# Linear memory over two blocks of 256 prompt tokens with a carried state, in place of one block of 512

## The chip, the cores and the metric

The kernel runs on one core of a Trainium2 chip. A core has a matrix engine (TensorE, PE in the profile; its weight loads are shown apart as PEld), a vector engine (VectorE, DVE), an activation engine (ScalarE, ACT), a general engine (GpSimd, POOL) and SyncE (SP), which here only issues transfers. TensorE writes to a small memory of its own, PSUM, of which this kernel uses one pool of four buffers for side work ("aux") and another for the large products ("mm"). The metric is the device time of one execution, in microseconds (us); the smaller the better.

## The reference

The kernel computes one layer of a streaming encoder for 512 prompt frames and 64 sample frames at width 1024: a feed-forward half step, a mixer of two branches, another feed-forward half step. One of the branches is a linear memory with four heads of 256. The reference runs it over chunks with a state C (256 x 256), n and a running maximum m:

```python
bcum = jnp.cumsum(lf, axis=-1)
dmat = jnp.where(causal, bcum[..., :, None] - bcum[..., None, :] + li[..., None, :], -jnp.inf)
inter = bcum + m[..., None]
m_t = jnp.maximum(inter, jnp.max(dmat, axis=-1))
w_inter = jnp.exp(inter - m_t)
s = jnp.einsum('bhtd,bhsd->bhts', q, k) * jnp.exp(dmat - m_t[..., None])
num = w_inter[..., None] * jnp.einsum('bhtd,bhde->bhte', q, C) + jnp.einsum('bhts,bhse->bhte', s, v)
den = w_inter * jnp.einsum('bhtd,bhd->bht', q, n) + jnp.sum(s, axis=-1)
h = num / jnp.maximum(jnp.abs(den), jnp.exp(-m_t))[..., None]
...
decay = jnp.exp(b_last + m - m_new)
w_s = jnp.exp(g_s - m_new[..., None])
C_new = decay[..., None, None] * C + jnp.einsum('bhs,bhsd,bhse->bhde', w_s, k, v)
```

The chunk length is free: any split of the tokens gives the same h and the same last state, since what the earlier chunks hold reaches a later one through C and n. The prompt starts with C = 0; the 64 sample frames bring a state of their own. After this h is normalised over the 256 entries of a head, gated, and multiplied by the branch's output matrix.

## The kernel before, in words

All products are done in three passes. A float32 operand is split in a high part (rounded to the matmul's float32 form, fp32r) and the remainder; `mm3` (L137) issues high x high, high x low and low x high as three matmuls into one PSUM bank. So each product of two tensors needs four tiles: for W they are Wh and Wl, for the keys kwh and kwl, for v vh and vl. The high part is mostly written by ScalarE (L147), the low part by VectorE (a subtraction, L150 or L153).

Tokens lie in blocks of 128: blocks 0 to 3 are the prompt, block 4 the 64 sample frames. The heads' loop (`for h in range(4)`) does for every head:

- `ml_kq` (L1986): the projections of k and q (four "gemms" of 24 matmuls a row half, weights streamed from memory), each followed by a short convolution over time on VectorE (U) and a SiLU on ScalarE (qf). `turn5` transposes k and v by TensorE, five blocks at a time, four in one aux bank and the sample's in the next; the sinks write kwh, kwl (scaled by the token's weight) and vh, vl. The v turns wait until the hidden blocks of the head before have been issued, since vh and vl have one buffer.
- `ml_decay` (L2035): the row of running maxima is spread over all partitions by two matmuls (mr, sel), copied to Mb, and ScalarE makes the decays D of each block by an exponential, masked by GpSimd. The exponential is in another function table than SiLU, so a table load stands between them.
- `ml_early`, `weights(b)`: for key block b the scores against all queries from that block on, W = (k q) * D. Over 512 prompt tokens these are 512, 384, 256 and 128 columns wide for b = 0 to 3, six matmuls each, and 64 for the sample.
- `ml_late`: `state(e)` sums k and v over the four prompt blocks (12 matmuls of 258 columns: 256 of v, one of ones for n, one unused) and over the sample block (3), for each half e of the key dimension. `hidden(b)` multiplies W and v: for block b one term from each of the blocks 0 to b, three matmuls a term, and the result is copied to hf by ScalarE. The sample's has one term and two of the old state (ch, cl, with q scaled in qsc). Then `norm` on hf, and `back(e)` transposes hf and multiplies by the gate og.

The order on TensorE is written out by hand. `Order` (L42 to L84) holds a clock that every matmul advances by its estimated length; `later(dt, fn)` puts a piece of side work on a heap with a due time, and between the gemms' matmuls the pieces that are due are issued, with a space of 380 ns between two of them in the heads. So the side work of one head falls among the gemms of the same and the next head, and the due times (`10000 + 2100 * b` and the like) set where. After head 3 come the projections of three branch gates (FILL), then what is left on the heap, then gate 7 and the output matrix of the branch. The order of the other engines comes from a scheduler that takes the emitted order and priorities (`high_priority`, `hot`); each engine runs its list strictly in turn.

The four aux banks are handed out in rotation by `bank()` (L122): a request waits until the last reader of the buffer four requests ago is done.

Before the heads, `gate_rows` (L1391) computes the sums of the forget gates, the running maxima and the exponentials for all heads on four partitions, in small pieces among the attention's projections (about 430 to 530 us in the profile). It ends by transposing the 128-row tile `rows` into `tcol`, which holds per token and head the columns: a weight for D, a weight for the keys, exp(-m).

Of the kernel before, what the change touches and what calls it, by code (L numbers as in the profile page):

```python
# [17 lines left out]
P = 128  # L18
# [68 lines left out]
def tile_layer(ctx: ExitStack, tc: tile.TileContext, ins, outs):  # L87
# [1274 lines left out]
    scol = gp.tile([4, 8], F32, name="scol")  # L1362
    tcol = gp.tile([P, 5, 12], F32, name="tcol")
    tstack = ExitStack()
# [16 lines left out]
    POOL.memset(tcol[:, 4, :], 1.0)  # L1381
    gdone = []
    vf0, kf0, qf0 = (slot(F32, tp, t) for t in ("vf0", "kf0", "qf0"))

# [6 lines left out]
    def gate_rows():  # L1391
# [25 lines left out]
        SP.dma_start(outs["m"][:, 1:2], mt[:, T - 1:T])  # L1417
        for i, (a, b) in enumerate(((0, NP_), (NP_, T))):
            ts(scol[:, 4 + i:5 + i], mrow[:, b - 1:b], -1.0, None, ALU.mult)
            yield act(rows[32:36, a:b], arow[:, a:b], AF.Exp, bias=scol[:, 4 + i:5 + i])  # L1420
# [9 lines left out]
        for b in range(5):  # L1430
            w = min(P, T - b * P)
            ps = bank()
            transpose(ps[:w, :P], rows[:, b * P:b * P + w], ident)
            yield DVE.tensor_copy(tcol[:w, b, :].rearrange("p (g h) -> p g h", h=4),
                                  ps[:w, :96].rearrange("p (g r) -> p g r", r=32)[:, :, 0:4])
        gdone.append(1)
# [598 lines left out]
    def ml_decay(h, st):  # L2035

        mb, mb2 = bank(), bank()
        pick = sel[:, h:h + 1].to_broadcast([P, P])
        mm(mb, pick, mr[:, :NP_], True, True)
        mm(mb2[:, 0:130], pick, mr[:, NP_:], True, True)  # L2040
        Mb = mp.tile([P, T], F32, tag="Mb", name=nm("Mb"))
        wdb = mp.tile([P, 66], F32, tag="wdb", name=nm("wdb"))
        with tc.high_priority(offset=120):
            act(Mb[:, :NP_], mb)
            act(Mb[:, NP_:], mb2[:, 0:64])
            act(wdb, mb2[:, 64:130])
# [8 lines left out]
        D = st["D"] = {}  # L2055

        def decays():

            for b in (4, 0, 1, 2, 3):
                s0 = b * P  # L2060
                n, w = (NP_ - s0, P) if b < 4 else (NS, NS)
                d = D[b] = mp.tile([P, n], F32, tag=f"D{b}", name=nm("D"))
                with tc.issue_after(order["silu"].ins):
                    order["exp"] = act(d[:w, :], Mb[:w, s0:s0 + n], AF.Exp, scale=-1.0, bias=tcol[:w, b, h:h + 1])

                POOL.affine_select(out=d[:w, 0:w], in_=d[:w, 0:w], pattern=[[1, w]], compare_op=ALU.is_ge, fill=0.0,
                                   base=0, channel_multiplier=-1)
            with tc.issue_after(order["exp"].ins):
                act(ch, c0v)
            tt(cl, c0v, f(ch), ALU.subtract)  # L2070

        later(6000, decays)

    def ml_early(h, st):
# [15 lines left out]
        def weights(b):  # L2090
            s0 = b * P
            n, w = (NP_ - s0, P) if b < 4 else (NS, NS)
            ps, d = bank(), D[b]
# [15 lines left out]
        for b in range(5):  # L2109

            later(10000 + 2100 * b if h == 3 else 11000 + 2600 * b, lambda b=b: weights(b))

    def ml_late(h, st):
        W, (c0, ch, cl), wdb, qs_ = st["W"], st["C"], st["wdb"], st["qs"]
        mv = mp.tile([P, 5, 2], F32, tag="mv", name=nm("mv"))
        dn = mp.tile([P, 5, 2], F32, tag="dn", name=nm("dn"))

        def state(e):

            ce = slice(e * P, (e + 1) * P)  # L2120
# [6 lines left out]
            SP.dma_start(outs["pC"][h, :, e, :], cn)  # L2127
            ps = bank()
            mm3(ps[:, :258], kwh[:, 4, ce], kwl[:, 4, ce], vh[:, 4, :], vl[:, 4, :], True, True)
# [238 lines left out]
```

## Time and profile before

| | us |
|---|---|
| median of 3 runs | 1546.58 |
| lowest, highest | 1545.94, 1548.52 |
| the profiled execution | 1547.03 |
| its span, first to last instruction | 1544.8 |
| TensorE busy in it | 1528.6 |
| VectorE busy | 1170.6 |
| ScalarE busy | 880.9 |
| GpSimd busy | 197.2 |

The granted clock of TensorE was 0.999 of full speed in that execution. The lines of the profile shown below are from it. A line of the list of instructions reads: start in us from the beginning of the span, duration in us, engine, source line, operation, output tile <- input tiles, sizes, and how many like it follow each other; in square brackets, where the engine stood idle before it, for how long and what ended it. TensorE's matmuls overlap: the distance from one start to the next is the pace, the duration is longer. L133 is the helper that issues matmuls, L143 transposes, L147 ScalarE's activations, L150, L153 and L157 VectorE's two-operand and scalar operations. Tile names carry no numbers, and an instruction is known by the tiles that it writes and reads: `aux<-qk,s` are the scores of `weights`, `aux<-vh,W` hidden blocks, `aux<-vh,kwh` the state, `aux<-ident,vf` a turn of v, `aux<-ident,qf` a turn of k, `aux<-ident,hf` the turn back, `mm<-...` the gemms.

### The profile page before, as it was taken

Reading aid. Unit: us, or ns where it says so; the run is one execution under the profiler, and the core shown is the slowest. Engines: PE = TensorE matmul, PEld = TensorE weight load, DVE = VectorE, ACT = ScalarE, POOL = GpSimd, SP = SyncE. Lnnn points to the kernel's source line nnn. Section 1 sums busy time; section 2 is a strip of 40 time slices with the busy share of each in tenths; the row PEclk is TensorE's granted clock in tenths of the full one; section 3 lists DMA queues with packets and bytes.
Section 4 is the critical chain, followed back from the end, with each engine's and each line's share of the span. In section 5 each row is a group of like instructions: output and inputs, shape, how many; then the busy total and the mean of one; then the engine's idle time right before and its main releaser. Section 6 shows DMA issues by size and latency. Waiting matters only on the chain.

```text
span 1544.8 us, 29439 instructions
## 1 busy us (share of the span) xinstructions
PE 1528.6 (99%) x11563; PEld 1513.4 (98%) x11563; DVE 1170.6 (76%) x2222; ACT 880.9 (57%) x1684; POOL 197.2 (13%) x370
## 2 busy tenths in 40 slices
PE   9999999999999999999999999999999999999998
PEld 9999999999999999999999999999999999999997
DVE  7877778776898767887677577775788888787765
ACT  7545446534666557777864877753456454557332
POOL 1000000100200015544200321102120000001000
PEclk9999999999999999999999999999999999999999
DMA  8322223524544449687544965542653223217333
GB/s 246 109 104 89 96 96 102 144 81 142 150 145 148 145 176 234 151 212 165 140 108 154 275 152 131 130 132 83 202 121 104 109 83 110 83 66 188 88 110 113
DMA packets 81075, 209.23 MB, mean 135 GB/s; under 512 B 9385, under 2 KB 23081, under 8 KB 80937
## 3 DMA queue, kind: packets, MB, share of 16 engines
q1 hardware_dynamic: 64936, 168.36, 32.2%
q0 software_dynamic: 14848, 37.30, 13.5%
q8 instruction: 90, 1.47, 0.4%
q10 hardware_dynamic: 1152, 1.70, 0.3%
q14 instruction: 49, 0.39, 0.1%
HBM read 170.89 MB, written 22.22 MB: 125 GB/s over the span
## 4 chain that ended last, share of the span: by engine, by line
PE 79%; DVE 9%; ACT 5%; DMA 3%; issue 3%; POOL 1%; SPq 0%; ACTq 0%; DVEq 0%; POOLq 0%
PE mm L133 67%; PE aux L133 11%; PE aux L143 1%; DVE wl L150 1%; ACT wh L147 1%; DMA s<-in_xT 1%; DVE s L150 1%; DVE sc L1608 1%; DVE s L153 1%; DVE o L150 1%; DVE U L153 1%; ACT sc L147 1%; DVE sc L157 1%; DMA wr<-in_w_in 1%; DVE kl L150 1%
## 5 line engine op out<-in xcount | busy, mean ns | idle before, releaser
L133 PE MATMUL mm<-s,wh 128*128 128x288 f32 (+2 forms) x3494 | 713.4, 298 | 1.0 <-DVE s L150 0.7
L133 PEld LDWEIGHTS mm<-s,wh 128*128 128x128 f32 x3494 | 558.7, 189 | 3.8 <-issue 0.9
L133 PE MATMUL mm<-s,wl 128*128 128x288 f32 (+2 forms) x1737 | 512.7, 295 | 0.0
L133 PEld LDWEIGHTS mm<-s,wl 128*128 128x128 f32 x1737 | 327.1, 188 | 0.2 <-DVE wl L150 0.2
L147 ACT ACTIVATE wh<-wr 128x1024 fp32r<-128x1024 f32 (+2 forms) x126 | 116.8, 935 | 108.3 <-PE mm L133 59.8
L133 PE MATMUL mm<-tx,wh 128*128 128x288 f32 x778 | 158.4, 296 | 0.0
L133 PEld LDWEIGHTS mm<-tx,wh 128*128 128x128 f32 x778 | 124.9, 188 | 0.0
L150 DVE TENSOR_TENSOR wl<-wr,wh 128x1024 fp32r<-128x1024 f32 (+2 forms) x87 | 90.8, 1053 | 36.6 <-ACT wh L147 36.5
L133 PE MATMUL mm<-tx,wl 128*128 128x288 f32 x383 | 113.0, 295 | 0.7 <-DVE wl L150 0.7
L976 ACT ACTIVATE wh<-wt 128x1024 fp32r<-128x1024 f32 x53 | 56.2, 1060 | 88.9 <-DVE wt L150 88.9
L150 DVE TENSOR_TENSOR wl<-wt,wh 128x1024 fp32r<-128x1024 f32 x53 | 64.8, 1222 | 52.6 <-ACT wh L976 52.6
L150 DVE TENSOR_TENSOR wl<-wu,wh 128x1024 fp32r<-128x1024 f32 x50 | 61.2, 1223 | 21.6 <-ACT wh L976 21.6
L223 POOL DMA_DIRECT2D s<-s x16 | 13.7, 855 | 495.0 <-ACT s L147 252.1
L133 PEld LDWEIGHTS mm<-tx,wl 128*128 128x128 f32 x383 | 72.0, 188 | 0.9 <-DVE wl L150 0.9
L147 ACT ACTIVATE h<-h 128x288 f32<-128x288 f32 x80 | 34.9, 437 | 65.2 <-DVE h L150 65.1
L976 ACT ACTIVATE wh<-wu 128x1024 fp32r<-128x1024 f32 x50 | 52.9, 1058 | 32.7 <-PE mm L133 32.5
L150 DVE TENSOR_TENSOR wl<-ws,wh 128x1024 fp32r<-128x1024 f32 x53 | 64.6, 1219 | 0.1
L150 DVE TENSOR_TENSOR ws<-wu 128x1024 f32<-128x1024 f32 x53 | 64.5, 1216 | 0.0
L133 PE MATMUL mm<-h,wh 128*128 128x256 f32 (+2 forms) x296 | 60.2, 294 | 0.0
L976 ACT ACTIVATE ah<-wu 128x512 fp32r<-128x512 f32 x53 | 33.4, 631 | 44.4 <-PE mm L133 41.3
L976 ACT ACTIVATE wh<-ws 128x1024 fp32r<-128x1024 f32 x53 | 55.8, 1052 | 0.7 <-PE mm L133 0.4
L147 ACT ACTIVATE sc<-sc,mx 128x128 f32<-128x128 f32 (+4 forms) x72 | 40.3, 560 | 25.1 <-DVE mx L1608 24.7
(420 smaller groups left out, 3609.0 us busy)
## 6 DMA issues: line engine op xcount, KB each, us to landing
wu<-in_w_gu SPq DMA_DIRECT2D x80, 512.0 KB, 4.4
wr<-in_w_in SPq DMA_DIRECT2D x46, 512.0 KB, 4.1
wl<-in_w_in POOLq DMA_DIRECT2D x38, 512.0 KB, 6.5
wr<-in_w_dn SPq DMA_DIRECT2D x34, 512.0 KB, 3.5
wu<-in_w_in SPq DMA_DIRECT2D x26, 512.0 KB, 4.7
wr<-in_w_dn SPq DMA_DIRECT2D x18, 384.0 KB, 3.5
s<-s POOLq DMA_DIRECT2D x16, 288.0 KB, 3.8
wr<-in_w_ap SPq DMA_DIRECT2D x8, 512.0 KB, 3.5
```

What stands on the lines that cost most here:

```text
L133: PE.matmul(out, lhsT, rhs, start=start, stop=stop, **kw)
L143: PE.transpose(out, in_, idn)
L147: return ACT.activation(out, in_, func, **kw)
L150: return (eng or DVE).tensor_tensor(out, a, b, op=op)
L153: return DVE.scalar_tensor_tensor(out=out, in0=a, scalar=s, in1=b, op0=op0, op1=op1)
L157: return (eng or DVE).tensor_scalar(out=out, in0=a, scalar1=s1, scalar2=s2, op0=op0, **kw)
L223: return POOL.dma_start(lo, src, accum_op=ALU.add)
L976: self.last = ACT.activation(hi, src, AF.Copy)
L1608: DVE.tensor_tensor_reduce(out=out, in0=ps, in1=g, op0=ALU.add, op1=ALU.min, scale=-1.0, scalar=3e38, accum_out=acc)
```

## The change

The prompt is treated as two blocks of 256 tokens (NC = 256). Within a block the scores and hidden products are as before, so the weights are 256 and 128 columns wide in each of the two blocks, and a hidden block has one or two terms. What the first 256 tokens give to the second goes through the state: `first(e)` sums k and v over token blocks 0 and 1 into cf, which is split into cfh and cfl; `carried(b)`, for b = 2 and 3, multiplies the queries by it (6 matmuls of 258 columns) and ScalarE copies the result to hc with a factor per token; hidden 2 and 3 add hc as they leave PSUM, on VectorE. The final state is g * cf plus the sum over token blocks 2 and 3 (`second(e)`), with the factor g from one more exponential a head; the sample's part of the state is a piece of its own (`sample(e)`). In `gate_rows` the weights of the keys are taken relative to the maximum at the end of their own block, the factor per token is one more exponential of 256 columns, and `tcol` and its copies are 16 wide rather than 12 (the copy reads 128 columns rather than 96).

The pieces' due times change too: scores and hidden blocks come later, and state sums are six pieces a head in place of two.

```diff
-    tcol = gp.tile([P, 5, 12], F32, name="tcol")
+    tcol = gp.tile([P, 5, 16], F32, name="tcol")
...
+    NC = NP_ // 2
...
-        for i, (a, b) in enumerate(((0, NP_), (NP_, T))):
+        yield act(rows[96:100, NC:NP_], mrow[:, NC:NP_], AF.Exp, bias=mrow[:, NC - 1:NC], scale=-1.0)
+        for i, (a, b) in enumerate(((0, NC), (NC, NP_), (NP_, T))):
             ts(scol[:, 4 + i:5 + i], mrow[:, b - 1:b], -1.0, None, ALU.mult)
             yield act(rows[32:36, a:b], arow[:, a:b], AF.Exp, bias=scol[:, 4 + i:5 + i])
...
             for b in (4, 0, 1, 2, 3):
                 s0 = b * P
-                n, w = (NP_ - s0, P) if b < 4 else (NS, NS)
+                n, w = (NC - s0 % NC, P) if b < 4 else (NS, NS)
...
+            with tc.issue_after(order["exp"].ins):
+                order["exp"] = act(g, Mb[:, NP_ - 1:NP_], AF.Exp, scale=-1.0, bias=Mb[:, NC - 1:NC])
...
         def weights(b):
             s0 = b * P
-            n, w = (NP_ - s0, P) if b < 4 else (NS, NS)
+            n, w = (NC - s0 % NC, P) if b < 4 else (NS, NS)
...
-            later(10000 + 2100 * b if h == 3 else 11000 + 2600 * b, lambda b=b: weights(b))
+            later(11200 + 2000 * b if h == 3 else 12600 + 2500 * b, lambda b=b: weights(b))
...
-        def state(e):
+        def first(e):
             ce = slice(e * P, (e + 1) * P)
             ps = bank()
-            for s in range(4):
-                mm3(ps[:, :258], kwh[:, s, ce], kwl[:, s, ce], vh[:, s, :], vl[:, s, :], s == 0, s == 3)
+            for s in range(2):
+                mm3(ps[:, :258], kwh[:, s, ce], kwl[:, s, ce], vh[:, s, :], vl[:, s, :], s == 0, s == 1)
+            with tc.high_priority(offset=100):
+                act(cf[:, e, :], ps[:, :258])
+            act(cfh[:, e, :], cf[:, e, :])
+            tt(cfl[:, e, :], cf[:, e, :], f(cfh[:, e, :]), ALU.subtract)
+
+        def second(e):
+            ce = slice(e * P, (e + 1) * P)
+            ps = bank()
+            for s in range(2, 4):
+                mm3(ps[:, :258], kwh[:, s, ce], kwl[:, s, ce], vh[:, s, :], vl[:, s, :], s == 2, s == 3)
             cn = mp.tile([P, 258], F32, tag="cn", name=nm("cn"), bufs=2)
             with tc.high_priority(offset=100):
-                act(cn, ps[:, :258])
+                stt(cn, cf[:, e, :], st["g"][:, 0:1], ps[:, :258], ALU.mult, ALU.add)
             SP.dma_start(outs["pC"][h, :, e, :], cn)
...
+        def carried(b):
+            ps = bank()
+            for e in range(2):
+                qh, ql = (x[:, b * P:(b + 1) * P] for x in st["q"][e])
+                mm3(ps[:, :258], qh, ql, cfh[:, e, :], cfl[:, e, :], e == 0, e == 1)
+            with tc.high_priority(offset=100):
+                act(hc_[:, b - 2, :], ps[:, :258], scale=tcol[:, b, 12 + h:13 + h])
...
-                          vh[:, s, :], vl[:, s, :]) for s in range(b + 1)]
+                          vh[:, s, :], vl[:, s, :]) for s in range(b // 2 * 2, b + 1)]
...
             with tc.high_priority(offset=60):
-                act(hf_[:w, b, :], ps[:w, :258])
+                if b in (2, 3):
+                    tt(hf_[:, b, :], ps[:, :258], hc_[:, b - 2, :], ALU.add)
+                else:
+                    act(hf_[:w, b, :], ps[:w, :258])
...
         for e in range(2):
-            later(5500 + 1800 * e, lambda e=e: state(e))
+            later(4500 + 1300 * e, lambda e=e: first(e))
+            later(7000 + 2400 * e, lambda e=e: second(e))
+            later(8200 + 2400 * e, lambda e=e: sample(e))
+        for b in (2, 3):
+            later(14000 + 2000 * (b - 2) if h == 3 else 16300 + 2600 * (b - 2), lambda b=b: carried(b))
         for b in range(5):
-            later(16000 + 1800 * b if h == 3 else 19500 + 2200 * b, lambda b=b: hidden(b))
+            later(17000 + 1800 * b if h == 3 else 20500 + 2200 * b, lambda b=b: hidden(b))
```

More of the change, by code (lines that the diff above doesn't have):

```diff
@@ L1434, in gate_rows @@
             yield DVE.tensor_copy(tcol[:w, b, :].rearrange("p (g h) -> p g h", h=4),
-                                  ps[:w, :96].rearrange("p (g r) -> p g r", r=32)[:, :, 0:4])
+                                  ps[:w, :P].rearrange("p (g r) -> p g r", r=32)[:, :, 0:4])
         gdone.append(1)
@@ L2055, in ml_decay @@
         D = st["D"] = {}
+        st["g"] = g = mp.tile([P, 1], F32, tag="g", name=nm("g"), bufs=2)
         def decays():
@@ L2116, in ml_late, with sample @@
         dn = mp.tile([P, 5, 2], F32, tag="dn", name=nm("dn"))
-        def state(e):
+        cf = mp.tile([P, 2, 258], F32, tag="cf", name=nm("cf"))
+        cfh, cfl = (mp.tile([P, 2, 258], F32R, tag=t, name=nm(t)) for t in ("cfh", "cfl"))
+        hc_ = mp.tile([P, 2, 258], F32, tag="hc", name=nm("hc"))
+        def first(e):
             ce = slice(e * P, (e + 1) * P)
             ps = bank()
-            for s in range(4):
-                mm3(ps[:, :258], kwh[:, s, ce], kwl[:, s, ce], vh[:, s, :], vl[:, s, :], s == 0, s == 3)
+            for s in range(2):
[9 more added lines that the diff above has]
+                mm3(ps[:, :258], kwh[:, s, ce], kwl[:, s, ce], vh[:, s, :], vl[:, s, :], s == 2, s == 3)
             cn = mp.tile([P, 258], F32, tag="cn", name=nm("cn"), bufs=2)
             with tc.high_priority(offset=100):
-                act(cn, ps[:, :258])
+                stt(cn, cf[:, e, :], st["g"][:, 0:1], ps[:, :258], ALU.mult, ALU.add)
             SP.dma_start(outs["pC"][h, :, e, :], cn)
+        def sample(e):
+            ce = slice(e * P, (e + 1) * P)
             ps = bank()
```

## The prediction

> **What bounds the kernel now.** I read the page first (busy shares, then the chain), then the table by stretches over the heads, then the lists of single instructions of TensorE, ScalarE and VectorE at the places the change touches.
>
> ```profile
> PE 1528.6 (99%) x11563; PEld 1513.4 (98%) x11563; DVE 1170.6 (76%) x2222; ACT 880.9 (57%) x1684; POOL 197.2 (13%) x370
> ...
> PE 79%; DVE 9%; ACT 5%; DMA 3%; issue 3%; POOL 1%; SPq 0%; ACTq 0%; DVEq 0%; POOLq 0%
> ```
> ```profile
> 860.00:900.00 40.00, 39.84 (x306) 39.21 (x305) 27.18 (x55) 33.88 (x77) 8.69 (x22) 1.00 0.94 255
> 900.00:950.00 50.00, 50.00 (x392) 49.31 (x391) 37.37 (x106) 38.94 (x93) 10.05 (x27) 1.00 0.52 125
> 950.00:1000.00 50.00, 50.00 (x389) 49.48 (x387) 38.05 (x101) 35.43 (x83) 10.35 (x26) 1.00 0.54 130
> 1000.00:1040.00 40.00, 40.00 (x311) 39.72 (x311) 27.70 (x63) 23.60 (x46) 2.83 (x6) 1.00 0.47 145
> ```
>
> TensorE is busy 99% of the span and 79% of the chain. In the second block (columns: length, then the busy time of TensorE, its weight loads, VectorE, ScalarE and GpSimd, the granted clock, the DMA share) the four heads lie between about 860 and 1040 us: TensorE stands still there for 0.16 of 180 us, at a clock of 1.00, while VectorE is busy 130.3 and ScalarE 131.9 of the 180. So a nanosecond of TensorE saved in the heads counts in full, and so does a wait put in front of one of its instructions. What the other engines gain or lose counts only through such a wait. Order on TensorE is fixed by hand; a wait there holds up everything behind it, the projections' gemms too.
>
> **What the change takes off TensorE.** It issues as many matmuls as before. Hidden blocks 2 and 3 lose two terms each (12 matmuls of 258 columns a head); the two carried products add 12 of 258. The state's 12 of 258 are only split in two groups of six. Nothing there. The weights of blocks 0 and 1 become narrower: six matmuls of 512 columns become 256, six of 384 become 128; blocks 2 and 3 stay. Their pace, from the start of the six to the start of what follows:
>
> ```profile
> 887.30 1.57 PE L133 MATMUL aux<-qk,s 128*128 128x512 f32 x6
> 888.70 0.40 PE L133 MATMUL mm<-s,wh 128*128 128x256 f32 x2
> ...
> 890.22 1.20 PE L133 MATMUL aux<-qk,s 128*128 128x384 f32 x6
> 891.26 0.46 PE L133 MATMUL mm<-s,wh 128*128 128x320 f32 x2
> ...
> 893.01 0.84 PE L133 MATMUL aux<-qk,s 128*128 128x256 f32 x6
> 893.69 0.46 PE L133 MATMUL mm<-s,wh 128*128 128x320 f32 x2
> ...
> 895.71 0.78 PE L133 MATMUL aux<-qk,s 128*128 128x128 f32 x6
> 896.33 0.46 PE L133 MATMUL mm<-s,wh 128*128 128x256 f32 x2
> ```
>
> 1.40 us for six of 512, 1.04 for 384, 0.68 for 256, 0.62 for 128 (the last two nearly alike: below 256 columns the pace hardly falls). A head saves (1.40 − 0.68) + (1.04 − 0.62) = 1.14 us, the four heads 4.6 us. That is the whole gain on the bounding engine.
>
> [...]
>
> **What the change adds beside TensorE.** Per head ScalarE gets cf and cfh twice, hc twice and g once in place of cn twice and hf twice, and its exponentials and W copies become narrower; VectorE gets cfl, cn and the sum hf twice each, against narrower D and W. Each is 0.3 to 0.5 us, by the rows of hf, W and D below. Per head that is some 1 to 1.5 us more on VectorE and about nothing on ScalarE; with a quarter of their time idle they cost nothing by their length. GpSimd's triangle masks keep their number and width, and SP issues the same DMAs; the one of the state leaves 1.5 us of order time later and now waits for VectorE. The weight loads queue behind it on SP; no row of TensorE in the heads waits for a load, so I take nothing.
>
> What can cost is that TensorE now meets products and banks earlier. The four aux buffers go round; the fifth request waits until the reader of the first is done. I compared, request by request, the distance to that reader before and after, in the changed order of each engine; a distance is the sum of the matmuls between, at the paces of the rows (0.12 us at 256 or 258 columns, 0.147 at 320, 0.11 for a transpose). These are the places where it gets too short.
>
> *Weights of block 2, head 0.* Weights of block 1, the carried product and the two decay matmuls come just ahead, so the group takes the buffer that weights of block 1 left 0.44 + 0.72 + 0.44 + 0.30 + 0.35 = 2.25 us earlier. Its reader, the product D on VectorE, stands in order behind two convolution steps, the low half of W and the low half of k:
>
> ```profile
> 889.71 1.68 DVE L153 SCALAR_TENSOR_TENSOR U<-R,cols,U 128x579 f32<-128x579 f32 x2
> ...
> 894.62 0.76 DVE L153 SCALAR_TENSOR_TENSOR s<-qf,s 128x576 fp32r<-128x576 f32 x1 [0.69 <-ACT s L147]
> ...
> 896.67 0.42 DVE L150 TENSOR_TENSOR W<-D,W 128x256 fp32r<-128x256 f32 x1 [0.48 <-ACT W L147]
> ...
> 899.36 0.28 DVE L150 TENSOR_TENSOR D<-aux,D 128x128 f32<-128x128 f32 x1
> ```
>
> 1.68 + 0.42 + 0.76 + 0.28 = 3.1 us and about 0.2 until a matmul's result stands (the last of six ends 0.16 after the next begins): 3.3 − 2.25 = 1.1 us of wait. It may be 0 (VectorE had 0.69 and 0.48 idle here) or 1.7. A wait of the same kind for hidden block 1 just behind it: 0.15 us (0 to 0.5).
>
> *Hidden block 2, head 0.* It takes the buffer of hidden block 0, which ended 2.37 us before; that eviction stands on ScalarE behind the table load for the decays:
>
> ```profile
> 901.34 0.63 ACT L147 ACTIVATE qf<-U 128x512 f32<-128x512 f32 x1 [0.58 <-DVE U L153]
> ...
> 902.46 1.28 ACT L147 ACT_TABLE_LOAD   x1
> 903.75 0.72 ACT L147 ACTIVATE D<-Mb,tcol 128x512 f32<-128x512 f32 x1
> 904.38 0.67 ACT L147 ACTIVATE s<-qf 128x576 fp32r<-128x576 f32 x1
> 904.96 0.36 ACT L147 ACTIVATE R<-mm 128x256 f32<-128x256 f32 x1
> 905.22 0.36 ACT L147 ACTIVATE kwh<-aux,tcol 128x128 fp32r<-128x128 f32 x1
> 905.47 0.66 ACT L147 ACTIVATE hf<-aux 128x258 f32<-128x258 f32 x2
> ```
>
> From the load's start to the end of the first hf 3.4 us, 3.15 with D at half its width; with part of qf ahead of it 3.8: 3.8 − 2.37 = 1.4 us. It is 0 if the load was through by then, 2.7 if the whole load comes on top. In the other heads that eviction stands ahead of the load, and 0.9 us are left. [...]
>
> *The two v turns, three times.* Hidden 4 comes later, and the turns of v wait for it. The second now starts 1.2 us behind the first, and its last 64-row transpose takes the first's buffer 1.62 us after that one's transposes began. Before, the second came 2.6 to 4.2 us later:
>
> ```profile
> 908.12 0.71 PE L143 MATMUL aux<-ident,vf 128*128 128x128 f32 x5
> ...
> 910.72 0.71 PE L143 MATMUL aux<-ident,vf 128*128 128x128 f32 x5
> ```
> ```profile
> 909.84 0.87 DVE L150 TENSOR_TENSOR vl<-aux,vh 128x512 fp32r<-128x512 f32 x2
> ...
> 913.63 0.67 DVE L150 TENSOR_TENSOR vl<-aux,vh 128x512 fp32r<-128x512 f32 x1
> ```
>
> The reader vl of the four blocks is done at 909.84 + 0.67 = 910.5, 2.4 us after the first turn's start; at the second turn at 914.3, 3.6 us after. 2.4 − 1.62 = 0.8; I take 0.73 each, a little under that row, 2.2 us in all. The lower end is vl straight behind its copy vh: some 0.8 to the first result, 0.5 for vh and 0.67 for vl leave 0.3 each, 0.9 in all; the upper one is 3 × 1.96 = 5.9.
>
> *The end of head 3.* With nothing more to come the norm of the last head is covered only by gemms. Between hidden 4 and the turn back stood 24 matmuls of 256 and 24 of 320 columns, 6.4 us; in the changed order stand 6 and 24, 4.2 us.
>
> ```profile
> 1026.34 0.28 PE L133 MATMUL aux<-ch,qsc 128*64 128x258 f32 x1
> 1026.45 0.40 PE L133 MATMUL mm<-s,wh 128*128 128x256 f32 x2
> ...
> 1032.41 0.46 PE L133 MATMUL mm<-s,wh 128*128 128x320 f32 x2
> ...
> 1032.85 1.25 PE L143 MATMUL aux<-ident,hf 128*128 128x128 f32 x10
> ```
> ```profile
> 1026.53 1.23 DVE L150 TENSOR_TENSOR wl<-wr,wh 128x1024 fp32r<-128x1024 f32 x1 [0.32 <-ACT wh L147]
> 1027.67 0.16 DVE L153 SCALAR_TENSOR_TENSOR dn<-hf,tcol 128x5 f32<-128x5 f32 x1
> ...
> 1030.57 1.70 DVE L157 TENSOR_SCALAR hf<-hf,mv,mrs 128x256 f32<-128x256 f32 x5
> ```
>
> The norm took from 1026.62 to 1032.27, 5.65 us, of which about 0.6 was the weight split wl ahead of dn; that split stands earlier now, so about 5.05. TensorE gets there after 4.24 − 0.16 = 4.1 us. The wait is 1.0 if the turn needs all five blocks, 0.5 as it needs them one by one: 0.75 us (0.4 to 1.5).
>
> *The gate rows.* One more exponential there; in ScalarE's order the eviction of one projection half now stands behind a weight copy, and TensorE's group at 493.48 takes its buffer:
>
> ```profile
> 492.09 0.41 ACT L147 ACTIVATE st<-mm 128x288 f32<-128x288 f32 x1 [0.43 <-PE mm L133]
> 493.65 1.06 ACT L976 ACTIVATE wh<-wt 128x1024 fp32r<-128x1024 f32 x1 [1.15 <-DVE wt L150]
> ```
>
> Left at these times the eviction would end at 495.0, 1.5 us late; as ah moves behind the table load, the copies before it run some 1 us earlier: 0.5 us (0 to 1.5).
>
> **Sum.** 1.1 + 0.15 + 1.4 + 2.2 + 0.75 + 0.5 = 6.1 us of waits against 4.6 saved: +1.5 us. The profiled execution took 1547.03 us (span 1544.8) and the median of the three runs is 1546.58, so the sum gives 1548.5 for such an execution and 1548.1 for a median. I count 0.2%, 3.1 us, as what a measurement can tell from no change.
>
> **Rivals.**
> - *The saving comes through.* If VectorE and ScalarE run ahead of the places I gave them, as the idle 0.69 and 0.48 suggest for VectorE, only the tail and a part of the v turns remain, the lower ends, 1.3 us: 1546.6 − 4.6 + 1.3 = 1543.3. Against it: 2.25, 2.37 and 1.62 us of distance are under the length of the work that stands in order between. Under 1.5 us of waits in all it is faster.
> - *The v turns wait long.* VectorE has the norm, kwl and a convolution between the two turns, and its vl of the second turn in the rows above took 3.6 us after the transposes. If the first one's takes as long, each turn waits 2.0 us in place of 0.73: +3.7, 1551.8. It decides from 1.3 us a turn.
> - *The other waits near their upper ends* (table load 2.7, gate rows and tail 1.5 each): +1.3 + 1.0 + 0.75, 1551.1; slower once they add 1.6. Nothing in the rows ties the three together.
> - *A smaller saving.* If weight loads set the pace wherever gemm matmuls lie around, width counts only as from 256 to 128 columns, 0.06 us for six and 128 columns: 4 × 0.06 a head, 1.0 us in all, and 1546.6 + 6.1 − 1.0 = 1551.7. The 1.40 and 1.04 us rows speak against it. [...]
>
> **How the numbers follow.** Forecast of about no change 0.44, saving through 0.18, long v turns 0.22, other upper ends 0.12, smaller saving 0.04. So faster 0.18, same 0.44, slower 0.38. All waits at their lower ends (1.3) give 1543.3, at their upper ends (13.8) 1555.8; that all come together is unlikely, and the range ends at 1552.5, past the long turns.
>
> **What the profile after would show.** Right: the weights groups at about 0.7 and 0.62 us for six; TensorE busy less by some 4.6 us; idle of TensorE ahead of weights block 2 and hidden block 2 between heads 0 and 1, ahead of each second v turn's last transpose, and ahead of the last turn back. Wrong: those groups start without a gap (then faster); or waits on weight loads or on the carried product's split cfl, which I put at nothing because some 12 us of gemms lie between its making and its use.

## The result and the profile after

| | before | changed |
|---|---|---|
| median of 17 runs, us | 1548.52 (1545.94 to 1552.43) | 1550.86 (1548.46 to 1552.32) |
| span of the profiled execution, us | 1544.8 | 1548.8 |
| TensorE busy, us | 1528.6 | 1526.3 |

The ratio of the times is 1.0016, with a 95% interval of 1.0009 to 1.0024: 2.5 us slower (1.4 to 3.7), where +1.5 us was forecast and 0.2% counted as no change. The 1546.58 us on which the forecast stood was the median of the first three runs; what compares is the ratio.

First the page of the changed kernel and its table by stretches over the heads (length, then busy time of TensorE, its weight loads, VectorE, ScalarE and GpSimd, granted clock, DMA share, GB/s).

```profile
PE 1526.3 (99%) x11563; PEld 1510.6 (98%) x11563; DVE 1175.0 (76%) x2247; ACT 880.3 (57%) x1698; POOL 198.4 (13%) x370
...
PE 78%; DVE 10%; ACT 6%; issue 4%; DMA 2%; POOL 1%; SPq 0%; DVEq 0%; ACTq 0%; POOLq 0%
```
```profile
860.00:900.00 40.00, 39.34 (x305) 39.03 (x304) 27.08 (x59) 33.02 (x78) 9.31 (x22) 1.00 0.95 251
900.00:950.00 50.00, 48.15 (x385) 47.57 (x384) 38.23 (x102) 36.65 (x91) 9.37 (x23) 1.00 0.54 132
950.00:1000.00 50.00, 48.00 (x381) 47.15 (x381) 39.93 (x112) 37.26 (x94) 10.13 (x28) 1.00 0.53 131
1000.00:1040.00 40.00, 39.93 (x315) 39.28 (x314) 28.41 (x77) 21.85 (x44) 4.26 (x8) 1.00 0.44 130
```

TensorE is busy 2.3 us less over the whole execution, and it stands idle for 4.6 of these 180 us, where it had stood for 0.16. VectorE is busy 3.4 us more in the 180 and ScalarE 3.1 less; over the whole execution it is 4.4 more and 0.6 less, since the same 180 us hold not quite the same instructions in both kernels. The gain is there, and it is more than eaten by waits. In TensorE's list of the changed kernel (in brackets the idle time and what ended it):

```profile
897.03 0.98 PE L133 MATMUL aux<-qk,s 128*128 128x256 f32 x6 [0.66 <-DVE D L150]
...
906.94 0.39 PE L133 MATMUL aux<-vh,W 128*128 128x258 f32 x1 [1.25 <-ACT hf L147]
...
915.41 0.30 PE L143 MATMUL aux<-ident,vf 128*64 128x128 f32 x1 [0.60 <-DVE vl L150]
...
957.68 0.30 PE L143 MATMUL aux<-ident,vf 128*64 128x128 f32 x1 [1.00 <-DVE vl L150]
...
999.60 0.30 PE L143 MATMUL aux<-ident,vf 128*64 128x128 f32 x1 [1.00 <-DVE vl L150]
...
1035.30 1.98 PE L143 MATMUL aux<-ident,hf 128*128 128x128 f32 x10
```

Five waits and one stretched group: weights of block 2 and hidden block 2 of head 0, the last transpose of the second v turn at each of three transitions, and the ten transposes of the last turn back, which took 1.98 us for 1.25. An idle time leaves out the tail of the matmul before, so I also use the distance from each start to the next, less the median for that form of matmul: 0.82, 1.41, 0.76, 1.16, 1.16 and 0.70 us. I call the sum of these distances beyond the median, over all matmuls between 855 and 1062 us, the excess of the heads (good to about 0.1). It was 2.3 us before and is 7.8 now. And I compare the same stretch of program, from TensorE's 6,290th to its 8,000th matmul (before head 0's state sums to the branch's output matrix): 222.6 us before, 224.8 now. Both are worked out from the traces.

The span's 4.0 us are more than the 2.5 of the runs, and the place of the rest is known: 1.0 us near 403 us, where instructions are the same in both kernels, and 0.4 near 1446 us.

```profile
403.62 0.81 PE L133 MATMUL aux<-dg,one 128*128 128x320 f32 x2 [1.13 <-DVE dg L157]
```

In the eleven experiments below, the excess around this first place lay anywhere between 0.6 and 2.1 us, and 0.04 to 0.3 around the second (0.7 and 1.1 in the two traces compared), with no edit near them: that is how one execution differs from another. The stretch of program leaves it out.

### The profile page after: what moved, and what is told of

Its sections match the earlier page's. It is cut to its first block, busy times and chain, and to the rows that moved or that the text cites. A ratio compares the mean times of both kernels' runs of the same rounds, so it can differ in the third digit from the quotient of the medians.

```text
span 1548.8 us, 29469 instructions
## 1 busy us (share of the span) xinstructions
PE 1526.3 (99%) x11563; PEld 1510.6 (98%) x11563; DVE 1175.0 (76%) x2247; ACT 880.3 (57%) x1698; POOL 198.4 (13%) x370
## 4 chain that ended last, share of the span: by engine, by line
PE 78%; DVE 10%; ACT 6%; issue 4%; DMA 2%; POOL 1%; SPq 0%; DVEq 0%; ACTq 0%; POOLq 0%
PE mm L133 66%; PE aux L133 10%; DVE wl L150 1%; PE aux L143 1%; DVE sc L1610 1%; DVE U L153 1%; DVE s L153 1%; DVE s L150 1%; DVE sc L157 1%; ACT wh L147 1%; ACT L147 1%; DVE o L150 1%; ACT sc L147 1%; ACT s L147 1%; DVE ptl L150 1%
## 5 line engine op out<-in xcount | busy, mean ns | idle before, releaser
L147 ACT ACTIVATE s<-s 128x576 fp32r<-128x576 f32 (+5 forms) x89 | 46.9, 555 | 13.7 <-DVE s L150 7.0
```

The source lines that it names most:

```text
L147: return ACT.activation(out, in_, func, **kw)
```

## The experiments

The theory after the traces: the saving on TensorE is real, and the loss is a sum of separate waits, each at a bank whose reader stands too far back in another engine's order. The main rival: VectorE has one backlog in this stage, and a wait mended in one place comes back in another. In the table, what the traces gave. The times of runs follow in the text where there were three rounds. The others ran once: carried_first 1550.13, evict_first 1550.55, gate_exp_late 1548.41, wide_weights 1553.37 and due_times_only 1550.55 us, where the median of the kernel before was 1546.95 in the same rounds, and vl_first 1550.74, copy_x3 1548.43 and copy_x5 1549.27, where one run of it took 1548.12. Runs of the kernel before lay between 1545.1 and 1550.1 in these rounds, so a single time decides little, and I go by the gaps in the traces.

| run | heads' excess, us | stretch, us |
|---|---|---|
| before | 2.3 | 222.6 |
| changed | 7.8 | 224.8 |
| turns_apart | 8.3 | 224.8 |
| turns_apart_h | 4.3 | 221.3 |
| carried_first | 8.0 | 224.9 |
| evict_first | 7.5 | 224.6 |
| vl_first | 7.4 | 224.4 |
| five_waits_off | 2.6 | 219.8 |
| wide_weights | 7.7 | 228.5 |
| due_times_only | 8.1 | 228.4 |
| copy_x3 | 7.9 | 224.9 |
| copy_x5 | 8.6 | 225.0 |
| gate_exp_late | 8.3 | 225.1 |

The last row shows what a single trace is worth. That edit lies far ahead of the heads, and there the other engines' instructions stand in the same order as in the changed kernel; yet the excess is 0.5 and the stretch 0.4 us more, as the gap ahead of weights of block 2 was 1.20 for 0.82. In the six runs whose edit is not aimed at this gap and whose waits near it are otherwise alike (turns_apart_h, evict_first, vl_first, gate_exp_late, copy_x3, copy_x5) it lay between 0.62 and 1.28. So differences of 0.5 us between rows of the table say nothing by themselves; the gap that an edit aims at does.

### The two v turns apart

```diff
-            def v_turn(vf, sink):
+            def v_turn(vf, sink, wait):
                 if hid[0] < 5 * h:
-                    later(300, lambda: v_turn(vf, sink))
+                    later(300, lambda: v_turn(vf, sink, wait))
+                elif wait:
+                    later(wait, lambda: v_turn(vf, sink, 0))
                 else:
                     turn5(vf, sink)
-            later(7500 + 6500 * e, lambda vf=vf, s=v_sink, fn=v_turn: fn(vf, s))
+            later(7500 + 6500 * e, lambda vf=vf, s=v_sink, fn=v_turn, wt=2600 * e: fn(vf, s, wt))
```

> One edit to the changed kernel: the second v turn waits 2600 ns of order time after the first (it comes 4.1 us behind instead of 1.2). Bank theory: the three gaps ahead of the second turn's 64-row transpose (0.76, 1.16 and 1.16 us in the changed kernel) vanish, nothing else moves, and TensorE's excess over its paces in the heads falls from 7.8 to about 4.7 us; time about 3 us less, 1547.5 to 1548 where the changed kernel has 1550.9, equal to the kernel before or 0.1% under it. Rival, VectorE is simply behind in this stretch: the second turn is late anyway and its vl is then late for the state sums or the turn back, so 1.5 us or more of the 3.1 come back there.

The median of nine runs was 1549.65 us, ratio 1.0019 (1.0009 to 1.0030). The three gaps at the v turns were gone, and yet nothing was gained. The edit also moved the turn of head 0, where no hidden block holds it up, and there it came too late for the state sums. What the edit cost, 2.9 and 0.8 us of waits and some 1.5 us of slow matmuls, was about what went: the 3.1 at the v turns, 0.8 ahead of weights of block 2 and 1.0 ahead of hidden block 2, which TensorE now reached later. The list of TensorE and the table by stretches of that run:

```profile
884.05 0.38 PE L133 MATMUL aux<-vh,kwh 128*128 128x258 f32 x1 [2.72 <-ACT vh L147]
884.96 0.58 PE L133 MATMUL aux<-vl,kwh 128*128 128x258 f32 x1 [0.53 <-DVE vl L150]
885.34 0.42 PE L133 MATMUL aux<-vh,kwl 128*128 128x258 f32 x1
885.56 0.42 PE L133 MATMUL aux<-vh,kwh 128*128 128x258 f32 x1
```
```profile
884.00:886.00 2.00, 1.42 (x6) 1.23 (x7) 1.96 (x6) 1.10 (x2) 0.60 (x1) 0.73 0.81 314
886.00:888.00 2.00, 2.00 (x10) 2.00 (x10) 1.20 (x3) 1.08 (x3) 0.24 (x1) 0.50 0.54 55
...
890.00:892.00 2.00, 2.00 (x18) 2.00 (x17) 2.00 (x6) 1.83 (x5) 0.64 (x2) 1.00 0.15 47
```

The edit made a new wait of 2.9 us, and behind it the granted clock was 0.50 and a matmul of 258 columns took 0.22 us for 0.12. Neither theory had that. So I repeated the edit with `wt=2600 * e * (h > 0)`.

> As turns_apart, but only from the second head on: in the first head the delayed turn had come after the state sums wanted it (TensorE waited 2.9 us there and then ran its matmuls at about 214 ns for 120 for some 3 us). Bank theory: the three gaps ahead of the second turns' last transpose (3.1 us) stay away and the wait in head 0 is gone; TensorE's excess in the heads falls from 7.8 to between 4.0 and 5.0 us, and the ratio to the kernel before falls to 0.9995 to 1.0005, from 1.0016 for the changed kernel. Rival: the wait moves on to the turn back or the state sums, and the excess stays above 6.5 us.

Ratio 0.9994 (0.9984 to 1.0003), ten runs, 1546.37 us against 1546.95. Excess 4.3 for 7.8, stretch 3.4 us shorter: the three gaps of 3.1 us went, and nothing came back at the turn back or the state sums. The backlog theory falls for this place. Moving the two turns apart is enough to put the changed kernel level with the one before.

### vl ahead in VectorE's order

In VectorE's list of the changed kernel, what stood between the first v turn's transposes (954.65) and the release of its bank at the second transition:

```profile
954.77 0.68 DVE L150 TENSOR_TENSOR cl<-c,ch 128x516 fp32r<-128x516 f32 x1
955.38 0.59 DVE L153 SCALAR_TENSOR_TENSOR kwl<-aux,tcol,kwh 128x128 fp32r<-128x128 f32 x2
...
955.99 0.78 DVE L153 SCALAR_TENSOR_TENSOR U<-R,cols,U 128x579 f32<-128x579 f32 x1
956.69 0.34 DVE L153 SCALAR_TENSOR_TENSOR kwl<-aux,tcol,kwh 128x128 fp32r<-128x128 f32 x1
956.95 0.87 DVE L150 TENSOR_TENSOR vl<-aux,vh 128x512 fp32r<-128x512 f32 x2
```

ScalarE had written vh from 955.29 to 955.89; vl began 1.06 us later, behind a convolution step and kwl. The edit raises only the priority of the v copies:

```diff
-    def turn5(src, sink):
+    def turn5(src, sink, off=100):
...
-            with tc.high_priority(offset=100):
+            with tc.high_priority(offset=off):
                 sink(b0, nb, w, ps[:w, :nb * P].rearrange("p (b c) -> p b c", c=P))
...
-                    turn5(vf, sink)
+                    turn5(vf, sink, 400)
```

> One edit to the changed kernel: the copies of v out of PSUM (vh, vl) get the priority 400 for 100, the turns stay 1.2 us apart; VectorE's order then has vl ahead of one kwl of 0.26 us. Theory (the gap is the place of vl in VectorE's order): each of the three gaps (0.76, 1.16, 1.16) shrinks by 0.2 to 0.5 us, none vanishes, since vh and the convolution step stay ahead. Rival, the gap is the turn of the bank itself, whatever the order: unchanged within 0.1.

```profile
957.98 0.30 PE L143 MATMUL aux<-ident,vf 128*64 128x128 f32 x1 [0.74 <-DVE vl L150]
```

The gaps were 0.51, 0.90 and 0.90: each shrank by 0.25 or 0.26, the one kwl of 0.26 us that vl now went past. The bank is free when vl is done (at the first transition of the changed kernel vl ended at 915.35 and the transpose started at 915.41), and vl's time is its place in the order. Of the 0.8 us the excess shows 0.4, as the gap ahead of weights of block 2 was 1.28 in this trace.

### The carried product ahead of the weights

```diff
-            later(14000 + 2000 * (b - 2) if h == 3 else 16300 + 2600 * (b - 2), lambda b=b: carried(b))
+            later(14000 + 2000 * (b - 2) if h == 3 else (11300, 18900)[b - 2], lambda b=b: carried(b))
```

> One edit to the changed kernel: in heads 0 to 2 the carried product of block 2 is issued ahead of weights of block 0 (due 11300 for 16300), so weights of block 2 find 4.4 us between themselves and the last use of their buffer, not 2.25. Bank theory: the 0.82 us gap ahead of weights of block 2 in head 0 vanishes (under 0.1), the 1.4 us gap ahead of hidden block 2 stays within 0.3. Rival, the gap is VectorE's late product itself: then the wait only moves to the next reader of that product (weights of block 3 or hidden block 1) and the excess of the heads stays at 7.8 within 0.3.

The gap ahead of weights of block 2 vanished, and that ahead of hidden block 2 was 1.48. But the heads' excess stayed at 8.0, the number of the rival, by another cause: the carried product came so early that its last matmul waited for the low half of q, which VectorE was still writing, 0.37 us. The other 0.6 us lay in small gaps, 0.20 of it at a turn of k before this place, which is about what one trace differs from another.

```profile
891.09 0.39 PE L133 MATMUL aux<-cfh,qk 128*128 128x258 f32 x1 [0.20 <-DVE qk L153]
```

A due time between weights of blocks 0 and 1 (13900) was left for the combination below, where this wait and that one are both absent.

### The copies of hidden blocks ahead

In ScalarE's list of the changed kernel, the copy of hidden block 0 out of its bank (hf), on which hidden block 2 waits, stood where the prediction had put it:

```profile
903.71 1.28 ACT L147 ACT_TABLE_LOAD   x1
905.00 0.51 ACT L147 ACTIVATE D<-Mb,tcol 128x256 f32<-128x256 f32 x1
905.41 0.67 ACT L147 ACTIVATE s<-qf 128x576 fp32r<-128x576 f32 x1
905.99 0.36 ACT L147 ACTIVATE R<-mm 128x256 f32<-128x256 f32 x1
906.25 0.36 ACT L147 ACTIVATE kwh<-aux,tcol 128x128 fp32r<-128x128 f32 x1
906.50 0.39 ACT L147 ACTIVATE hf<-aux 128x258 f32<-128x258 f32 x1
```

```diff
-            with tc.high_priority(offset=60):
+            with tc.high_priority(offset=400):
                 if b in (2, 3):
```

> One edit to the changed kernel: the copies of hidden blocks out of PSUM get a higher priority (400 for 60), which puts the copy of hidden block 0 in head 0 ahead of the k split, an R copy and a kwh copy, still behind the table load and one D. Theory (the 1.4 us gap ahead of hidden block 2 is that copy's place in ScalarE's order): 0.67 + 0.36 + 0.36 less the overlaps, about 1.1 us, of it goes, 0.3 is left for the load. [...]

The gap fell from 1.41 to 0.31 us, by the 1.1 of the three instructions passed. D started 0.02 us after the load's end (906.68; 0.01 in the changed kernel), and hf followed D. But 0.16 appeared at hidden block 3, and the v turn's gap of the same transition grew from 0.76 to 1.40. TensorE arrived earlier there, but VectorE's order had changed too: cl, 0.70 us, which stood behind both turns' vl in the changed kernel, now ran ahead of the first. Which of the two made the gap grow, this run doesn't part. Of 1.1 us gained 0.3 was left in the excess.

```profile
907.51 0.39 PE L133 MATMUL aux<-vh,W 128*128 128x258 f32 x1 [0.15 <-ACT hf L147]
...
916.88 0.30 PE L143 MATMUL aux<-ident,vf 128*64 128x128 f32 x1 [1.24 <-DVE vl L150]
```

Here the main rival is half right: two waits behind each other are not independent, through TensorE's time of arrival or through the other engine's order.

### The gate rows

In the changed kernel, TensorE's and ScalarE's lists:

```profile
494.83 0.53 PE L133 MATMUL mm<-s,ah 128*128 128x288 f32 x2 [0.20 <-ACT st L147]
```
```profile
493.42 1.06 ACT L976 ACTIVATE wh<-wt 128x1024 fp32r<-128x1024 f32 x1 [2.33 <-DVE wt L150]
494.39 0.39 ACT L147 ACTIVATE st<-mm 128x288 f32<-128x288 f32 x1
```

```diff
-        yield act(rows[96:100, NC:NP_], mrow[:, NC:NP_], AF.Exp, bias=mrow[:, NC - 1:NC], scale=-1.0)
...
-        yield act(wd[:, 64:65], mrow[:, T - 1:T], AF.Exp, bias=scol[:, 2:3], scale=-1.0)
+        wdl = act(wd[:, 64:65], mrow[:, T - 1:T], AF.Exp, bias=scol[:, 2:3], scale=-1.0)
+        yield wdl
+        with tc.issue_after(wdl.ins):
+            carry_exp = act(rows[96:100, NC:NP_], mrow[:, NC:NP_], AF.Exp, bias=mrow[:, NC - 1:NC], scale=-1.0)
+        yield carry_exp
```

> One edit to the changed kernel: the added exponential of the gate rows goes behind the other exponentials in ScalarE's order, which puts the projection's copy out of PSUM ahead of the weight copy again, as in the kernel before. Theory: the gap of 0.37 us ahead of the group near 494.8 us vanishes, and TensorE's excess between 440 and 560 us is that of the kernel before. Rival: the gap comes with the wider rows of the gate or chance, and stays.

The gap of 0.37 us vanished; the excess between 440 and 560 us was 0.59 for 1.05 in the changed kernel and 0.72 in the one before. One exponential of four partitions costs 0.4 us here by its place alone; the same trace has it in another place and no gap.

### The saving put back

```diff
             ps, d = bank(), D[b]
+            m, t0 = NP_ - s0 if b < 4 else n, od.now
             for e in range(2):
...
-                mm3(ps[:w, :n], kh[:, s0:s0 + w], kl[:, s0:s0 + w], qh[:, s0:s0 + n], ql[:, s0:s0 + n],
+                mm3(ps[:w, :m], kh[:, s0:s0 + w], kl[:, s0:s0 + w], qh[:, s0:s0 + m], ql[:, s0:s0 + m],
                     e == 0, e == 1)
+            od.now = t0 + 6 * (max(n / 2.4, w * 0.83) + 2)
```

> One edit to the changed kernel, in its exact order: the score matmuls of blocks 0 and 1 run over all 512 and 384 columns as in the kernel before, and the columns past the block's end are left unused (work that the change had removed, put back). Theory: 24 matmuls at 0.233 for 0.119 us and 24 at 0.174 for 0.112: 4.2 us more on TensorE, the gaps within 0.5 us of the changed kernel's in sum; about 1555. Rival, the narrow matmuls' saving is partly lost behind weight loads or waits: 2 us or less.

One execution took 1553.37 us, and the stretch 228.5 for 224.8, 3.7 us more. Hidden block 2, the v turns and the turn back waited as before the edit (1.41, 0.77, 1.16, 1.16, 0.70). The gap ahead of weights of block 2 was 0.13 for 0.82, presumably since wider matmuls gave VectorE time. So the matmuls themselves cost 3.7 us by this run, and 4.4 if that gap's fall is put down to them. In the traces of the kernels before and after, the groups of weights of 512 and 384 columns took 5.58 and 4.16 us for 24 matmuls each, and the added ones of 256 and 128 took 3.05 and 2.47: 4.2 us saved.

### Lateness alone

The kernel before, with only two lines of due times from the change:

```diff
-            later(10000 + 2100 * b if h == 3 else 11000 + 2600 * b, lambda b=b: weights(b))
+            later(11200 + 2000 * b if h == 3 else 12600 + 2500 * b, lambda b=b: weights(b))
...
-            later(16000 + 1800 * b if h == 3 else 19500 + 2200 * b, lambda b=b: hidden(b))
+            later(17000 + 1800 * b if h == 3 else 20500 + 2200 * b, lambda b=b: hidden(b))
```

> The kernel before with nothing but the changed kernel's due times for weights and hidden blocks (one block of 512, no carried product). Theory, lateness alone brings a part of the waits: behind head 0 hidden block 2 finds its buffer 1.6 us after the last use (it needs about 2.4) and the second v turn comes 1.2 us behind the first, so gaps of 0.5 to 1.2 us at each; in the two later transitions a turn of k stands between the v turns (2.3 us) and gaps are under 0.4; the last turn back waits 0.2 to 0.5. Excess in the heads 4 to 5.5 us for 2.3, about 2 to 3 us more than the kernel before. Rival, only the carried product's work brings the waits: excess under 2.8.

One execution took 1550.55 us; excess 8.1 us, well over the 4 to 5.5 that I expected. Lateness alone brings a gap of 0.77 at the first second v turn and 0.28 at the first turns of the later two transitions, as expected; no gap over 0.1 us at the last turn back, where I had 0.2 to 0.5. The surplus is at hidden block 2: a gap of 1.19 at the sample's scores, then 1.79, and then half the clock (third number from the end of a row).

```profile
900.63 0.54 PE L133 MATMUL aux<-qk,s 128*64 128x64 f32 x6 [1.02 <-DVE D L150]
...
903.31 0.58 PE L133 MATMUL aux<-vh,W 128*128 128x258 f32 x1 [1.63 <-DVE kwl L153]
```
```profile
903.40:905.00 1.60, 1.60 (x7) 1.60 (x8) 0.00 (x0) 1.59 (x4) 0.11 (x1) 0.50 0.16 31
905.00:906.60 1.60, 1.60 (x8) 1.60 (x8) 1.55 (x7) 1.60 (x7) 0.20 (x2) 0.52 0.00 0
906.60:908.00 1.40, 1.40 (x13) 1.40 (x12) 0.66 (x3) 1.24 (x5) 0.60 (x3) 1.00 0.00 0
```

So lateness alone can cost as much as the change loses, and at the first second v turn it brings the same gap (0.77, 0.76 in the changed kernel); but due times and what they move past can't be added up one by one.

### A longer wait

```diff
-                    act(hf_[:w, b, :], ps[:w, :258])
+                    for _ in range(3 if (h, b) == (0, 0) else 1):
+                        act(hf_[:w, b, :], ps[:w, :258])
```

> One edit to the changed kernel: ScalarE copies hidden block 0 of head 0 out of PSUM three times over in place of once (the same values), which holds its buffer longer; the two further copies and a W and a kwh copy that come between take about 1.0 us. Theory one (a wait costs its length): the 1.4 us gap ahead of hidden block 2 grows to about 2.4, everything behind it keeps its pace, excess in the heads 8.8. Theory two (after a wait over some 1.6 us TensorE's granted clock falls to a half, as in turns_apart after 2.7 us): the matmuls behind the gap run at about 214 ns for 120 for some 3 us, 1.5 us more, excess about 10.3 and a granted clock near 0.5 there.

> As copy_x3 with five copies: the gap grows to about 3.2 us. Theory one: excess 9.6. Theory two: half the pace behind the gap for as long as in copy_x3 or turns_apart (some 3 us, not longer for a longer gap), excess about 11.

Both missed. With three copies or five the gap grew only to 1.78 and 1.80 us, and the clock stayed at 1.00. With the longer hold hidden block 2 waited no more for hidden block 0 but for D, VectorE's reader of the sample's scores, so it had got another buffer:

```profile
906.33 0.39 PE L133 MATMUL aux<-vh,W 128*128 128x258 f32 x1 [1.64 <-DVE D L150]
```

The line is of copy_x5. So the buffers are not handed out in strict rotation, as I had described it ahead of the prediction: in the changed kernel too hidden block 2 waits for the third request before it, hidden block 0, and not for the fourth, weights of block 3. By what rule they are dealt out these runs don't show. What they do show is a single idle of 1.64 us without a slower clock; how a single idle of 2.4 us ends was not tried.

### All together

Five edits on the changed kernel: the v turns apart from the second head on, the carried product of block 2 at 13900, the priority of hidden's copies, the gate exponential behind the others, and for the last head

```diff
-            later(17000 + 1800 * b if h == 3 else 20500 + 2200 * b, lambda b=b: hidden(b))
+            later(15400 + 1600 * b if h == 3 else 20500 + 2200 * b, lambda b=b: hidden(b))
```

> The changed kernel with five edits of order together, all arithmetic as in it: the second v turn 2600 ns behind from the second head on, the carried product of block 2 between weights of blocks 0 and 1 (due 13900), the higher priority for the copies of hidden blocks, the last head's hidden blocks 1600 ns earlier and closer (15400 + 1600 b), the added exponential of the gate rows behind the others. Theory (the loss is the sum of separate waits, and the saving on TensorE is real): excess in the heads 2.8 to 3.5 us (2.3 in the kernel before), none of the 0.37 us in the gate rows, the saving of 4.2 us stays: 3 to 3.6 us under the kernel before, ratio 0.9975 to 0.9983. Rival, the waits are one backlog of VectorE that shows up elsewhere when a place is mended: excess 5 us or more and a ratio of 0.999 or above.

Ten runs, median 1544.0 us against 1546.95 for the kernel before: ratio 0.9977 (0.9967 to 0.9986). Excess 2.6 us; the largest gaps left are 0.55 at a turn of k, which waited 0.32 in the kernel before, and 0.39 at hidden block 2. The stretch took 219.8 us, 2.8 less than before. The table by stretches:

```profile
860.00:900.00 40.00, 39.61 (x309) 39.30 (x308) 26.88 (x58) 33.35 (x78) 8.97 (x21) 1.00 0.94 253
900.00:950.00 50.00, 49.75 (x394) 48.81 (x393) 39.55 (x110) 38.41 (x97) 10.29 (x27) 1.00 0.58 132
950.00:1000.00 50.00, 50.00 (x401) 49.93 (x399) 39.83 (x111) 37.47 (x91) 10.53 (x25) 1.00 0.57 134
1000.00:1040.00 40.00, 40.00 (x320) 39.94 (x320) 30.89 (x75) 24.29 (x50) 3.26 (x7) 1.00 0.47 140
```

With the same arithmetic as the change, and VectorE 3.5 us busier in these 180 than in the changed kernel (more of the program falls into them), TensorE stands idle for 0.6 us. It is the places, not the amount of work, that cost the change its gain. This kernel is faster than the kernel before, and by the ratios to that kernel faster than the changed one. What each of the five gives within it was not parted.

## Why the prediction was right, point by point

| step | forecast, us | measured, us |
|---|---|---|
| narrower weights | −4.6 | −4.2 |
| weights of block 2, head 0 | +1.1 | +0.82 |
| hidden block 1, head 0 | +0.15 | none |
| hidden block 2, head 0 | +1.4 | +1.41 |
| second v turns, three | +2.2 | +3.1 (0.76, 1.16, 1.16) |
| last turn back | +0.75 | +0.70 |
| gate rows | +0.5 | +0.37 |
| sum | +1.5 | +2.2 |

The places in the heads add up to +1.8, and the whole stretch is 2.2 us longer. The 0.4 between is the size of a wait just ahead of the heads that the prediction did not have:

```profile
844.23 1.06 ACT L147 ACTIVATE wh<-wr 128x1024 fp32r<-128x1024 f32 x1 [1.46 <-DMA wr<-in_w_in]
845.19 0.39 ACT L147 ACTIVATE o<-mm 128x288 f32<-128x288 f32 x1
```

TensorE's next group starts 0.30 us late at 845.63, after this copy o, and the matmul behind it 0.1 late; ScalarE had waited 0.72 us for that transfer in the kernel before. A delay of 0.24 to 0.47 us stands at this place in all eleven traces with the carried state and in neither of the two without; why the transfer comes later isn't shown. Small delays behind the waits (0.1 us each) and a gap of 0.32 at a turn of k that the change took away about cancel. With the gate rows the stretch gives +2.5, as the runs do (1.4 to 3.7). Each of the places of the table was named before, and no other gap of more than 0.12 us came in the heads.

That the sum came so near is in part luck. Too little was taken for the v turns (0.9) and too much saved (0.4), and four of the other terms were 0.05 to 0.3 too high.

- *The saving* was 0.4 too high. Three of the four groups of 256 columns in the kernel before took the 0.68 us of the row and one 0.71; all eight in the changed kernel took 0.71 or more, so the median is 119 ns a matmul in place of 113. Why isn't shown. The rival of a pace set by weight loads (1.0 us saved) is out: the medians in the heads were 233 ns a matmul at 512 columns (kernel before) and 112 at 128 (changed kernel).
- *The v turns* were the term mis-sized most, by 0.9 us. I took one value of 0.73 for all three. It held at the first transition; at the later two VectorE also had cl, 0.68 us, between the first turn and vl. The rival of long turns (2.0 us each) did not come, as no gap reached the 1.3 us at which it would have decided.
- *Weights of block 2* waited near the forecast time (0.82 for 1.1), but not on the work that was named. The two convolution steps were nearly through when weights of block 1 ended (893.84); in their place VectorE stood idle for 1.07 us, for a copy W that ScalarE wrote late, and only then came the low halves and the reader D. The place and the last part of the chain were right; that its first part came out as long was luck. VectorE's list of the changed kernel there:

```profile
893.88 0.42 DVE L150 TENSOR_TENSOR D<-aux,D 128x256 f32<-128x256 f32 x1
...
895.44 0.42 DVE L150 TENSOR_TENSOR W<-D,W 128x256 fp32r<-128x256 f32 x1 [1.07 <-ACT W L147]
896.02 0.76 DVE L153 SCALAR_TENSOR_TENSOR s<-qf,s 128x576 fp32r<-128x576 f32 x1
896.69 0.28 DVE L150 TENSOR_TENSOR D<-aux,D 128x128 f32<-128x128 f32 x1
```

- *The table load* acted as the row said: it took 1.28 us, the next instruction started at 905.00, 0.01 us after the load's end, and the wait ahead of hidden block 2 was 1.41 us. From the end of hidden block 0 to the end of its copy it took 3.8 us, as worked out.
- *The last turn back* showed not as one idle time ahead of it but as ten transposes at a slower pace (1035.30 to 1037.04), beside the norm's five blocks, which VectorE wrote from 1034.60 to 1036.30.
- *TensorE busy less by some 4.6 us*, named as a sign of being right, did not come: it was 2.3. The matmuls took 4.2 us less, but the tail of a matmul ahead of each wait (0.16) and the stretched turn back count as busy.
- *The rival on the other side*, that the saving comes through because the engines run ahead of their places, did not hold: they ran in the order given, and evict_first and vl_first show that a gap shrinks by the very instructions passed. But five_waits_off shows how near it was: with other places for the same work it is what happens.
- *The work put beside TensorE* (cf, cfh, cfl, hc, g, the sums) cost nothing by its length, as forecast; the state's transfers on SP neither, as no matmul of the heads waited for a load; the wait at 845.63, by way of ScalarE's weight copy, lies ahead of them.

## What to carry to other kernels

Where one engine is busy 99% and its order is fixed by hand, a change of 4 us in its work has to be judged by the distances between a buffer's last use and its next, against the work that stands ahead of its reader in the reader's own order: 2.3 to 2.4 us of distance were too little here; ahead of weights of block 2, 3.6 (five_waits_off) and 4.4 (carried_first) were enough, if their buffer was that of the fourth request before. When pieces move later, look first where two of them come to lie side by side on a short ring of buffers. And try the edits together, since one alone moves TensorE's arrival at the next wait, and the order of the other engines with it.

## What the runs showed of the hardware beyond that

In two of the runs the waits of TensorE cost more than their length. In turns_apart TensorE stood idle from 881.33 on for 3.2 of 3.6 us (2.72 in a row), and at 884.93 the granted clock fell to 0.50. In due_times_only it stood idle from 899.61 on for 2.5 of 3.5 us, never more than 1.45 in a row until then, and the clock fell at 903.13, still within the second wait. Both times it stayed at 0.50 for 3.4 us, and the matmuls of 258 columns ran at 0.215 us for 0.12, which lost about 1.5 us more. After single idles of 1.25 us (changed kernel) and 1.64 us (copy_x5), with no other close by, it stayed at 1.00. So it is not the single idle alone that decides; what does, these runs don't settle.
